# A conv-and-MLP trunk in split fp32 on one core: the activations' sums between stages are split in pieces from plain blocks, the input's gate product moves four steps

## The chip, the cores and the metric

The kernel runs on one core of one Trainium2 chip. Its time is device microseconds of that core, from one launch. The engines that matter are TensorE (PE for its matmuls, PEld for its weight loads), VectorE (DVE), ScalarE (ACT) and SyncE (SP), whose queue issues the DMAs. Every engine works through its own instructions in the order in which they were written; semaphores hold an instruction until what it needs is there.

## The reference

One layer: a gated short convolution and a squared-ReLU MLP, each after an RMS norm and added to the residual; 512 tokens, 2,048 channels, 8,192 hidden.

```python
h = rms_norm(x, norm_mix)
b_gate, c_gate, v = split(h @ conv_w_in, 3)          # 2048 x 6144
m = (b_gate * conv3(c_gate * v, conv_w)) @ conv_w_out # causal, depthwise, 3 taps
x = x + m
h = rms_norm(x, norm_mlp)
x = x + square(relu(h @ mlp_w1)) @ mlp_w2             # 2048 x 8192, 8192 x 2048
```

## The kernel before, in words

**Products.** Everything is fp32. Each operand is split into a high part, rounded to the type that PE multiplies in one pass, and a low part, the rest: `split` (L118) is a cast on ACT (L120) and a subtraction on DVE (L121). A product is three matmuls: high by high, high by low, low by high (L165 to L167 in plain blocks, L267 to L269 in fast blocks).

**Blocks and steps.** The output channels of each of the four weight matrices are worked off in blocks of 256 columns with 2,048 inputs. A *plain* block is 4 steps of 24 matmuls over 512 tokens each. A *fast* block is one level of Strassen-Winograd: inputs, outputs and tokens are halved, and 7 products of half size take the place of 8; it is 7 steps of 24 matmuls over 256 tokens each. Product by product the weights' quarters and sums are X11, S1, S2, S4, S3, X12, X22 (`quarters`, L169), and the activations' are Y11, T1, T2, Y22, T3, Y21, T4 (L33). In block 1 of a stage (`late`) the order is X11, X12, S2, S1, S3, S4, X22, so the activations' order is Y11, Y21, T2, T1, T3, Y22, T4.

The stages are `conv_w_in` (8 groups of the three parts C, V and B), `conv_w_out` (8 blocks), `mlp_w1` (32) and `mlp_w2` (4 times 8). The first, second and last block of `conv_w_in` behind the input, the first and last of `conv_w_out` and the first of `mlp_w1` are plain; the others are fast. There are 640 steps. Steps 0 to 3 and 4 to 7 are plain, 8 to 14 is the first fast block, (1,1) (group 1, part V); 141 to 144 is the last block of `conv_w_in`, 145 to 148 the first of `conv_w_out`; 191 to 194 its last, 195 to 198 the first of `mlp_w1`.

**Order.** It is written out by hand. At iteration i (L638 to L648) the kernel emits step i's matmuls, the copies out of PSUM of step i - 1 (`out`), the weight sums of step i + 3 (`add`), the weight split of step i + 2 (`operand`), and then what was put between steps with `at(i, ...)` (L203), in the order in which it was registered. So what is late on ACT or DVE in one iteration delays the copies and weights of the next ones. The products of a fast block add into three banks of PSUM; X11, S2, S3 and X22 share one, S1 and S4 another. The copy of one product must have left the bank before the next adds into it.

**Activations.** They lie in SBUF split, as quarters Y11, Y12, Y21, Y22 (`quart`), sums T2 and T4 (`sums`) and T3 (`last_sum`). T1 and Y12 share a place: plain blocks need all four quarters, fast blocks T1. Before a stage ends, its results go to DRAM by pairs of channel tiles (8 pairs), each with the four quarters and the four sums T1 to T4 (`differences`, L190; written by `keep`, L359). `pass_over` (L320) brings them into the next stage: with s the start of the last block and f that of the next stage's first, both plain, it reads and splits the quarters of pairs 0 to 6 (`fetch_pairs`, `settle_pairs`), takes the last pair's from its tile (`settle_last`), and then reads each sum as a whole, all eight pairs, from DRAM (`fetch`, L299) and splits it (`settle`, L304). Reads go into tiles of tag q, of which there are three; a read waits until its tile's last user is done, and SP's queue waits with it. The tag c, for a block's results, has two.

**The input.** While the first stage begins, the quarters are read back from DRAM (`fetch_h`, L570), normalised on ACT in eight operations (`normed_quarter`, L544), subtracted on DVE (`difference`, L574) and split (`settle_h`). `gate` (L389) multiplies a group's convolution by its B part on DVE, two operations of 1,024 columns, and appends the four sums (three operations); for group 0 that is registered for iteration 4. Y12, which the last block of `conv_w_in` needs again, is read 9 steps before it (L597).

In `residual` (L399) and `squared_relu` (L431) a finished block of `conv_w_out` or `mlp_w1` goes through DVE and ACT two iterations after its end. `token_factors` (L126) makes the second norm's factors: a matmul on PE at f + 2 = 197, then a chain on DVE with a square root on ACT.

Of the kernel before, what the change touches and what calls it, by code (L numbers as in the profile page):

```python
# [19 lines left out]
NP = KT // 2  # L20
# [3 lines left out]
NG = D // GC  # L24
# [8 lines left out]
Y11, T1, T2, Y22, T3, Y21, T4, Y12 = range(8)  # L33
PLACE = {Y11: 0, Y12: 1, Y21: 2, Y22: 3, T1: 4, T2: 5, T3: 6, T4: 7}
# [5 lines left out]
def trunk_kernel(  # L40
# [12 lines left out]
    nc = tc.nc  # L53
# [49 lines left out]
    sums = [cst.tile([P, 2, NP, HS], F32R, name=f"t_{n}") for n in ("hi", "lo")]  # L103
# [3 lines left out]
    def form(i):  # L107
        if i == T3:
            return last_sum
        return [quart[n][:, HOME[i]] if i in HOME else sums[n][:, i == T4] for n in range(2)]  # L110
# [7 lines left out]
    def split(hi, lo, src):  # L118

        act.copy(hi, src)  # L120
        dve.tensor_tensor(out=lo, in0=src, in1=hi.bitcast(F32), op=ALU.subtract)  # L121
# [68 lines left out]
    def differences(q):  # L190

        def tt(o, a, b):
            dve.tensor_tensor(out=q[:, o, :], in0=q[:, a, :], in1=q[:, b, :], op=ALU.subtract)

        tt(slice(4, 8, 2), slice(1, 4, 2), slice(0, 2))
        tt(5, 3, 4)
        tt(7, 2, 5)
# [5 lines left out]
    def at(i, fn, *args):  # L203
        between.setdefault(i, []).append((fn, args))
# [15 lines left out]
    def plain(w, r0, c0):  # L220
        box = new_block(w, r0, c0, KT // QK)

        def multiply(op, k0):
            if k0 == 0:
                box["acc"] = [bank() for _ in range(2)]
            plain_products(box["acc"], op, k0, k_first=True)

        def out(k0):
            if k0 == KT - QK:
                c = tile_c(box)  # L230
                for j in range(2):
                    act.copy(c[:, j, :], box["acc"][j])

        for k0 in range(0, KT, QK):
            steps.append((
                lambda: None,
                lambda k0=k0: plain_operand(box["r"], k0),
                lambda op, k0=k0: multiply(op, k0),
                lambda k0=k0: out(k0),
            ))  # L240
        return box
# [51 lines left out]
    def tile_q(name):  # L293
        return mw.tile([P, 8, HS], F32, tag="q", name=name, bufs=3)
# [22 lines left out]
    def settle_last(box):  # L317
        split(*(quart[i][:, :, NP - 1, :] for i in range(2)), box["q"][:, :4, :])

    def pass_over(last, first, src):  # L320


        s, f, box = last["start"], first["start"], {}
        at(s - 2, fetch_pairs, box, src, 0, 2)
        at(s, fetch_pairs, box, src, 2, 2)
        at(s + 1, settle_pairs, box, 0, 2)
        at(s + 1, fetch_pairs, box, src, 4, 2)
        at(s + 2, settle_pairs, box, 2, 2)
        at(s + 3, settle_pairs, box, 4, 2)
        at(s + 3, fetch_pairs, box, src, 6, 1)  # L330
        at(f, settle_pairs, box, 6, 1)
        at(f, settle_last, last)
        box = {}
        at(f + 1, fetch, box, src, T2)
        at(f + 2, fetch, box, src, T3)
        at(f + 3, settle, box, T2)
        at(f + 3, fetch, box, src, T1)
        at(f + 3, settle, box, T3)
        at(f + 3, fetch, box, src, T4)
        at(f + 4, settle, box, T1)  # L340
        at(f + 6, settle, box, T4)

    def exchange(start, src, reads):

# [11 lines left out]
    def tt(o, a, b, op):  # L356
        dve.tensor_tensor(out=o, in0=a, in1=b, op=op)  # L357
# [4 lines left out]
    def conv(n, box_c, box_v, d):  # L362

        e = box_v["end"]

        def product():
            tt(box_v["c"], box_c["c"], box_v["c"], ALU.mult)

        def factor():
            u = box_v["u"] = tile_x("u")  # L370
            dve.memset(u[:, :, 14:16], 0.0)
            tt(u[:, :, 16:], box_v["c"], wide(ssq), ALU.mult)

        def taps():
            u = box_v["u"]
            cv = box_v["cv"] = tile_x("cv")[:, :, :S]
            for j in range(2):
                act.activation(cv[:, j, :], u[:, j, 14 : 14 + S], AF.Copy, scale=tap(0, 2 * n + j))
                for i in (1, 2):
                    dve.scalar_tensor_tensor(  # L380
                        out=cv[:, j, :], in0=u[:, j, 14 + i : 14 + i + S], scalar=tap(i, 2 * n + j),
                        in1=cv[:, j, :], op0=ALU.mult, op1=ALU.add,
                    )

        at(e, product)
        at(e + d, factor)
        at(e + d + 1, taps)

    def gate(n, box_v, box, d):  # L389
        def product():  # L390
            q = box["q"] = tile_q("q")
            tt(box["c"], box["c"], box_v["cv"], ALU.mult)
            tt(q[:, :4, :].rearrange("p (i h) t -> p i (h t)", h=2), box["c"], wide(rbc), ALU.mult)

        at(box["end"] + d, product)
        at(box["end"] + d, lambda: differences(box["q"]))
        at(box["end"] + d + 1, keep, box, gated[n])
# [77 lines left out]
    with tc.tile_pool(name="xin", bufs=2) as xin:  # L475
# [18 lines left out]
        for c in range(D // XC):  # L494
# [5 lines left out]
            for i in range(2):  # L500
                src = w_in[c * XC : (c + 1) * XC, parts[i] : parts[i] + GC]
# [50 lines left out]
    for n in range(NG):  # L552
        trio = []
        for i in range(3):
            if n == 0 and i < 2:
                trio.append(boxes[i])
            elif (n, i) in ((0, 2), (1, 0), (NG - 1, 2)):
                trio.append(plain(w_in, 0, parts[i] + n * GC))
            else:
                trio.append(fast(w_in, 0, parts[i] + n * GC, late=(n, i) == (1, 1)))  # L560
            if i == 1:
                conv(n, *trio, 0 if n in (0, NG - 1) else 2)
        gate(n, *trio[1:], 0 if n in (0, NG - 1) else 2)
    in_last = trio[2]


# [1 line left out]
    hb = {}  # L568
# [17 lines left out]
    at(2, normed_quarter, hb, Y22)  # L586
    at(3, difference, Y12, Y22, Y12)
    at(3, settle_h, Y12, T3)
    at(4, difference, Y22, Y22, Y11)
    at(5, fetch_h, Y21)  # L590
    at(5, lambda: split(*form(T2), hb[Y22]))
    at(7, normed_quarter, hb, Y21)
    at(8, settle_h, Y11, T1)
    at(9, difference, Y21, Y21, Y22)
    at(10, settle_h, Y21, T4)

    at(in_last["start"] - 9, fetch_h, Y12)  # L597
    at(in_last["start"] - 6, normed_quarter, hb, Y12)
    at(in_last["start"] - 4, settle_h, Y12, Y12)


    for n in range(NG):
        if n in (0, NG - 1):
            box = plain(w_out, 0, n * GC)
        else:
            box = fast(w_out, 0, n * GC, late=n == 1)
        if n == 0:
            pass_over(in_last, box, gated)
        if n == NG - 1:
            back = {}  # L610
            at(box["start"] - 8, fetch, back, gated, Y12)
            at(box["start"] - 4, settle, back, Y12)
        residual(n, box, 0 if n >= NG - 2 else 2)


    for n in range(DFF // GC):
        last, box = box, fast(w1, 0, n * GC, late=n == 1) if n else plain(w1, 0, n * GC)
        if n == 0:
            pass_over(last, box, normed)
            at(box["start"] + 2, token_factors, lambda name: tile_x(name)[:, 0, :S])  # L620
        if n == DFF // GC - 1:
            exchange(box["start"], hidden[0], (-2, -1, 2, 3, 4, 5, 6))
        squared_relu(n, box)
    for ch in range(NCH):
        if ch:
            exchange(box["start"], hidden[ch], (-2, -1, 0, 2, 3, 4, 6))
        for n in range(NG):
            box = fast(w2, ch * D, n * GC)
# [53 lines left out]
```

## Time and profile before

| | us |
|---|---|
| median of 3 runs | 2005.88 (2002.95 to 2007.34) |
| the profiled execution | 2005.84 |
| its span, first to last instruction | 2004.1 |
| PE busy | 1932.6 (96%) |
| PEld busy | 1886.7 (94%) |
| DVE busy | 1650.9 (82%) |
| ACT busy | 979.5 (49%) |
| DMA | 355.79 MB, 178 GB/s on average |

In the page a matmul's duration overlaps its neighbours', so PE's busy time is not PE at its peak. The rows of a timeline give the start, the duration, the engine, the line of the kernel, the operation, what it writes and reads, and in brackets the engine's idle time before it with what ended it. The times of the 640 steps are not marked; they are found by the operands (q, t and u are `quart`, `sums` and `last_sum`) and the order above.

### The profile page before, as it was taken

The page shows a single profiled execution, that of the slowest core. Times are in us where ns is not written, and L with a number is a line of the kernel's source. Part 1 is how long each engine was busy: PE and PEld are TensorE (multiplying, and loading weights), DVE is VectorE, ACT ScalarE, POOL GpSimd, SP SyncE. Part 2 cuts the span into 40 slices and gives each one's busy share as a digit, 9 for nine tenths or more (in the row PEclk, how much of TensorE's full clock was granted, in tenths as well). Part 3 has the DMA queues.
Part 4 walks back from the last instruction along what each step waited for, and adds up shares of the span by engine and source line. Part 5 has one row for each costly group of instructions (what it writes and reads, how often), then busy time and mean ns, then how long its engine had stood idle before and what let it go on. Part 6 is the DMA issues. An engine that isn't in the chain of part 4 may idle for free. (4 is left out here: it accounts for less than half of the span.)

```text
span 2004.1 us, 36810 instructions
## 1 busy us (share of the span) xinstructions
PE 1932.6 (96%) x15729; PEld 1886.7 (94%) x15729; DVE 1650.9 (82%) x1686; ACT 979.5 (49%) x1232; POOL 0.7 (0%) x6
## 2 busy tenths in 40 slices
PE   9979999999989989999999999988999999999998
PEld 7769999999789879999999999988998998999998
DVE  6678988887688778888888888888889789879776
ACT  4544444444455544444544445454455446446443
POOL 0000000000000000000000000000000000000000
PEclk9999999999989989999999999999999999999999
DMA  8433433434755855445354453575556457548432
GB/s 273 168 126 112 142 130 103 148 106 170 266 184 198 306 177 171 152 165 180 136 190 152 164 181 135 190 250 177 183 198 243 159 188 265 178 149 291 161 136 96
DMA packets 279843, 355.79 MB, mean 178 GB/s; under 512 B 9520, under 2 KB 253312, under 8 KB 273536
## 3 DMA queue, kind: packets, MB, share of 16 engines
q1 hardware_dynamic: 279552, 353.41, 50.8%
q8 instruction: 123, 2.02, 0.4%
q14 instruction: 40, 0.33, 0.0%
q10 hardware_dynamic: 128, 0.04, 0.0%
HBM read 277.91 MB, written 75.50 MB: 176 GB/s over the span
## 5 line engine op out<-in xcount | busy, mean ns | idle before, releaser
L267 PE MATMUL acc<-q_hi,whi 128*128 128x256 f32 x2816 | 781.3, 277 | 4.0 <-ACT c L281 4.0
L269 PE MATMUL acc<-q_hi,wlo 128*128 128x256 f32 x2816 | 780.2, 277 | 2.6 <-DVE wlo L121 2.6
L268 PE MATMUL acc<-q_lo,whi 128*128 128x256 f32 x2816 | 780.5, 277 | 1.0 <-DVE q_lo L121 1.0
L121 DVE TENSOR_TENSOR wlo<-r,whi 128x1024 fp32r<-128x1024 f32 x384 | 469.2, 1222 | 232.2 <-ACT whi L120 222.6
L267 PEld LDWEIGHTS acc<-q_hi,whi 128*128 128x128 f32 x2816 | 531.1, 189 | 4.3 <-ACT c L281 4.2
L269 PEld LDWEIGHTS acc<-q_hi,wlo 128*128 128x128 f32 x2816 | 530.1, 188 | 3.1 <-DVE wlo L121 3.0
L268 PEld LDWEIGHTS acc<-q_lo,whi 128*128 128x128 f32 x2816 | 530.6, 188 | 1.9 <-DVE q_lo L121 1.8
L120 ACT CAST whi<-r 128x1024 fp32r<-128x1024 f32 x384 | 401.0, 1053 | 212.6 <-PE acc L268 115.8
L267 PE MATMUL acc<-t_hi,whi 128*128 128x256 f32 x1408 | 397.4, 282 | 32.8 <-DVE c L279 21.8
L269 PE MATMUL acc<-t_hi,wlo 128*128 128x256 f32 x1408 | 395.6, 281 | 2.2 <-DVE wlo L121 2.2
L268 PE MATMUL acc<-t_lo,whi 128*128 128x256 f32 x1408 | 395.5, 281 | 0.0
L120 ACT CAST whi<-s 128x1024 fp32r<-128x1024 f32 x264 | 278.4, 1055 | 206.0 <-DVE s L179 143.6
L121 DVE TENSOR_TENSOR wlo<-s,whi 128x1024 fp32r<-128x1024 f32 x264 | 322.3, 1221 | 25.9 <-ACT whi L120 22.2
L281 ACT COPY c<-acc 128x256 f32<-128x256 f32 x352 | 130.3, 370 | 402.2 <-PE acc L269 386.7
L267 PEld LDWEIGHTS acc<-t_hi,whi 128*128 128x128 f32 x1408 | 271.4, 193 | 35.1 <-issue 23.3
L269 PEld LDWEIGHTS acc<-t_hi,wlo 128*128 128x128 f32 x1408 | 270.9, 192 | 2.4 <-DVE wlo L121 2.4
L268 PEld LDWEIGHTS acc<-t_lo,whi 128*128 128x128 f32 x1408 | 271.1, 193 | 0.0
L267 PE MATMUL acc<-u_hi,whi 128*128 128x256 f32 x704 | 203.7, 289 | 13.5 <-ACT c L281 13.5
L268 PE MATMUL acc<-u_lo,whi 128*128 128x256 f32 x704 | 201.4, 286 | 1.3 <-DVE u_lo L121 1.3
L269 PE MATMUL acc<-u_hi,wlo 128*128 128x256 f32 x704 | 201.4, 286 | 0.0
L267 PEld LDWEIGHTS acc<-u_hi,whi 128*128 128x128 f32 x704 | 136.9, 195 | 14.7 <-ACT c L281 14.7
L268 PEld LDWEIGHTS acc<-u_lo,whi 128*128 128x128 f32 x704 | 137.0, 195 | 2.0 <-DVE u_lo L121 2.0
(76 smaller groups left out, 1796.7 us busy)
## 6 DMA issues: line engine op xcount, KB each, us to landing
r<-in_mlp_w_dram SPq DMA_DIRECT2D x256, 512.0 KB, 6.2
r<-in_conv_w_in_dram SPq DMA_DIRECT2D x96, 512.0 KB, 6.2
hidden<-q SPq DMA_DIRECT2D x32, 1024.0 KB, 4.3
f<-hidden SPq DMA_DIRECT2D x28, 1024.0 KB, 8.4
r<-in_conv_w_out_dram SPq DMA_DIRECT2D x32, 512.0 KB, 6.4
xt<-x_mid SPq DMA_DIRECT2D x32, 512.0 KB, 8.8
x_mid<-c SPq DMA_DIRECT2D x24, 512.0 KB, 2.6
gated<-q SPq DMA_DIRECT2D x8, 1024.0 KB, 3.8
```

What stands on the lines that cost most here:

```text
L120: act.copy(hi, src)
L121: dve.tensor_tensor(out=lo, in0=src, in1=hi.bitcast(F32), op=ALU.subtract)
L267: pe.matmul(acc, hi[:, k, :], f_hi[:, k, :], start=first, stop=False, skip_group_check=True)
L268: pe.matmul(acc, hi[:, k, :], f_lo[:, k, :], start=False, stop=False, skip_group_check=True)
L269: pe.matmul(acc, lo[:, k, :], f_hi[:, k, :], start=False, stop=last, skip_group_check=True)
L281: act.copy(o, acc)
```

## The change

Three parts.

1. In `pass_over`, pair 6 is read a step earlier in the order. Each sum is now read without its last pair (`fetch_most`: 7 of 8 pairs, one DMA of 896 KB), and split in two pieces: seven pairs from that read (`settle_most`) and the last pair from the tile in which it was made (`settle_rest`). Since the reads don't need the last pair in DRAM, they stand earlier: T2 at s + 3, T3 at f, T4 at f + 1, T1 at f + 2, in place of f + 1, f + 2, f + 3 (T1), f + 3 (T4). The splits stand at f + 1 (T2), f + 2 (T3), f + 3 (T4) and f + 4 (T1), in place of f + 3 (T2, T3), f + 4 (T1) and f + 6 (T4). The last pair's tile is in use until f + 4. This holds in both places that call `pass_over`.
2. At the input, Y21 is read at iteration 3 and not 5, and group 0's gate is registered for iteration 8 (its write to DRAM for 9) and not 4, behind T1's split.
3. Y12, before the last input block, is normalised and split one step later (5 and 3 steps before the block, not 6 and 4).

```diff
+    def fetch_most(box, src, i):
+        box[i] = tile_q("f")
+        nc.sync.dma_start(box[i][:, : NP - 1, :], src[: NP - 1, :, PLACE[i], :].rearrange("k p t -> p k t"))
+
+    def settle_most(box, i):
+        split(*(f[:, : NP - 1, :] for f in form(i)), box.pop(i)[:, : NP - 1, :])
+
+    def settle_rest(last, i):
+        split(*(f[:, NP - 1, :] for f in form(i)), last["q"][:, PLACE[i], :])
+
     def pass_over(last, first, src):
...
         at(s + 2, settle_pairs, box, 2, 2)
+        at(s + 2, fetch_pairs, box, src, 6, 1)
         at(s + 3, settle_pairs, box, 4, 2)
-        at(s + 3, fetch_pairs, box, src, 6, 1)
+        sums = {}
+        at(s + 3, fetch_most, sums, src, T2)
         at(f, settle_pairs, box, 6, 1)
         at(f, settle_last, last)
-        box = {}
-        at(f + 1, fetch, box, src, T2)
-        at(f + 2, fetch, box, src, T3)
-        at(f + 3, settle, box, T2)
-        at(f + 3, fetch, box, src, T1)
-        at(f + 3, settle, box, T3)
-        at(f + 3, fetch, box, src, T4)
-        at(f + 4, settle, box, T1)
-        at(f + 6, settle, box, T4)
+        at(f, fetch_most, sums, src, T3)
+        at(f + 1, settle_most, sums, T2)
+        at(f + 1, settle_rest, last, T2)
+        at(f + 1, fetch_most, sums, src, T4)
+        at(f + 2, settle_most, sums, T3)
+        at(f + 2, settle_rest, last, T3)
+        at(f + 2, fetch_most, sums, src, T1)
+        at(f + 3, settle_most, sums, T4)
+        at(f + 3, settle_rest, last, T4)
+        at(f + 4, settle_most, sums, T1)
+        at(f + 4, settle_rest, last, T1)
...
-        gate(n, *trio[1:], 0 if n in (0, NG - 1) else 2)
+        if n:
+            gate(n, *trio[1:], 0 if n == NG - 1 else 2)
+        else:
+            first_trio = trio
...
     at(3, settle_h, Y12, T3)
+    at(3, fetch_h, Y21)
     at(4, difference, Y22, Y22, Y11)
-    at(5, fetch_h, Y21)
     at(5, lambda: split(*form(T2), hb[Y22]))
     at(7, normed_quarter, hb, Y21)
     at(8, settle_h, Y11, T1)
+    gate(0, *first_trio[1:], 4)
     at(9, difference, Y21, Y21, Y22)
     at(10, settle_h, Y21, T4)

     at(in_last["start"] - 9, fetch_h, Y12)
-    at(in_last["start"] - 6, normed_quarter, hb, Y12)
-    at(in_last["start"] - 4, settle_h, Y12, Y12)
+    at(in_last["start"] - 5, normed_quarter, hb, Y12)
+    at(in_last["start"] - 3, settle_h, Y12, Y12)
```

## The prediction, made before the changed kernel ran

> **What bounds the kernel now.** I read the page first, then the stages' windows, then PE's timeline for its pauses, and last the timelines of ACT, DVE and SP around each pause. First the page's first line, then two windows of 300 and 3 us (columns: stretch, its length, busy time with count for PE, PEld, DVE, ACT, POOL, then granted clock, DMA share, GB/s).
>
> ```profile
> span 2004.1 us, 36810 instructions
> ```
>
> ```profile
> 150.00:450.00 300.00, 300.00 (x2627) 300.00 (x2626) 265.12 (x284) 140.21 (x185) 0.00 (x0) 1.00 0.36 124
> 552.90:555.90 3.00, 2.96 (x14) 2.96 (x15) 3.00 (x2) 0.94 (x1) 0.00 (x0) 0.50 0.08 29
> ```
>
> In the fast blocks PE never pauses: 300/2627 is 0.114 us a matmul, 2.73 us a step of 24; a plain step, 24 matmuls twice as wide, some 5.5. Right after a pause the clock is 0.50: 3/14 is 0.214 us a matmul. So time is to be had only where PE pauses. PE's timeline, the pauses that the change can reach (idle time in brackets):
>
> ```profile
> 110.26 0.50 PE L167 MATMUL acc<-q_hi,wlo 128*128 128x512 f32 x1 [1.51 <-DVE wlo L121]
> 128.64 0.58 PE L267 MATMUL acc<-t_hi,whi 128*128 128x256 f32 x1 [7.32 <-ACT c L281]
> 485.15 0.58 PE L267 MATMUL acc<-q_hi,whi 128*128 128x256 f32 x1 [3.98 <-ACT c L281]
> 552.94 0.58 PE L267 MATMUL acc<-t_hi,whi 128*128 128x256 f32 x1 [3.64 <-ACT c L281]
> 564.89 0.39 PE L267 MATMUL acc<-u_hi,whi 128*128 128x256 f32 x1 [3.39 <-ACT c L281]
> 727.46 0.39 PE L269 MATMUL acc<-q_hi,wlo 128*128 128x256 f32 x1 [2.40 <-DVE wlo L121]
> 744.82 0.58 PE L267 MATMUL acc<-u_hi,whi 128*128 128x256 f32 x1 [4.57 <-ACT c L281]
> ```
>
> They sum to 26.8 us, and a pause costs more than itself. Groups of L267, first in 673.3 to 676.0, then in 1668.3 to 1671.0, two pauses that the change leaves alone: after 2.1 us idle a matmul takes 286 ns, after 2.4 us it takes 449.
>
> ```profile
> L267 PE MATMUL acc<-t_hi,whi 128*128 128x256 f32 x8 | 2.3, 286 | 2.1 <-DVE c L279 2.1
> L267 PE MATMUL acc<-t_hi,whi 128*128 128x256 f32 x4 | 1.8, 449 | 2.4 <-DVE c L279 2.4
> ```
>
> The releaser "ACT c L281" is a copy out of PSUM: the next product adds into the same bank and must wait for it. ACT is in order, so a copy is late when something ahead of it waits.
>
> **The input.** DVE, then ACT, then SP:
>
> ```profile
> 102.75 1.22 DVE L357 TENSOR_TENSOR c<-c,cv 128x1024 f32<-128x1024 f32 x1
> 104.00 1.23 DVE L357 TENSOR_TENSOR q<-c,rbc 128x1024 f32<-128x1024 f32 x1
> 105.26 1.61 DVE L193 TENSOR_TENSOR q<-q 128x512 f32<-128x512 f32 x3
> 106.79 2.28 DVE L357 TENSOR_TENSOR f<-f 128x2048 f32<-128x2048 f32 x1
> 108.99 1.22 DVE L121 TENSOR_TENSOR wlo<-r,whi 128x1024 fp32r<-128x1024 f32 x1
> ...
> 136.50 1.22 DVE L121 TENSOR_TENSOR wlo<-r,whi 128x1024 fp32r<-128x1024 f32 x1
> ```
>
> ```profile
> 121.33 3.30 ACT L547 ACTIVATE f<-f,par 128x256 f32<-128x256 f32 x8 [8.36 <-DMA f<-x_res]
> ```
>
> ```profile
> 110.24 2.02 SPq L146 DMA_DIRECT2D r<-in_conv_w_in_dram  x4
> 112.36 0.48 SPq L572 DMA_DIRECT2D f<-x_res  x1
> ```
>
> Gate 0 (102.75 to 106.79, 4.04 us) stands ahead of step 7's low weights (108.99), and the read of Y21 stands behind four weight loads that wait for those; ACT waits 8.36 us for it, and with it the copies. With gate 0 gone from step 4, the low weights are done 4.04 us sooner, at 106.2; step 7 has no pause, and ends 1.7 sooner at 113.7 (110.26 + 22 x 0.23 - 1.7; to the idle time a little of matmul is added). Y21's read goes out when T3's low half frees its tile, just before the next low weights at 101.6; it is normalised before 113.7 if it lands within 8.7 us.
>
> Gate 0's new place brings a new wait. Tag c has two buffers, and the copy of block (1,1)'s X11 at iteration 9 wants the one that gate 0's product reads at iteration 8. From 113.9: two copies 1.0, S2's high weights 1.0, T1's high half 1.9 (117.75), its low half 2.29 (120.0), the product's two operations 1.25 each (122.5), the copy 0.37: step 10 (S2) starts at 122.9, where 119.2 (113.7 + 2 x 2.73) would be free and 128.64 was before. Behind that DVE runs differences 1.6, S3's addition 1.14, low weights 1.14, T4's difference 2.2, an addition 0.34, S4's addition 1.14, and reaches step 12's low weights (before: 136.50) at 130.0. **I take 6.5.** Low end 1.7 (only the first pause goes), high end 9.4 (the copy finds a free buffer).
>
> **Y12 before the last input block.** ACT, then PE:
>
> ```profile
> 481.55 3.30 ACT L547 ACTIVATE f<-f,par 128x256 f32<-128x256 f32 x8 [4.45 <-DMA f<-x_res]
> 484.75 0.35 ACT L281 COPY c<-acc 128x256 f32<-128x256 f32 x1
> ```
>
> ```profile
> 490.44 0.41 PE L267 MATMUL acc<-u_hi,whi 128*128 128x256 f32 x1
> ```
>
> The normalisation waits for its read, and S1's copy (484.75) behind it holds step 137. One step later, S1's copy is ahead of it; step 137 follows step 136 at once, and now S2's copy stands behind, at the same 484.75, and holds step 138 (S3) until 485.15 instead of 490.44: **5.3**. Behind 484.75 come the copy 0.27, two high weights 1.9, Y12's high half 1.9 and low half 2.3: 491.2; step 141 reads them from 485.15 + 3 x 2.73 = 493.3. Low end 2.7 (one step, if the rest keeps the half clock), high 6.9 (pause and half clock wholly gone).
>
> **First transition (f = 145).** SP, then the page's group of these reads (median us from issue to landing), then ACT and DVE:
>
> ```profile
> 532.28 0.37 SPq L302 DMA_DIRECT2D f<-gated  x1
> 532.70 0.61 SPq L403 DMA_DIRECT2D xt<-x_res  x1
> 533.41 3.82 SPq L146 DMA_DIRECT2D r<-in_conv_w_out_dram  x4
> 537.27 7.12 SPq L302 DMA_DIRECT2D f<-gated  x3
> ```
>
> ```profile
> f<-gated SPq DMA_DIRECT2D x5, 1024.0 KB, 9.7
> ```
>
> ```profile
> 547.00 1.91 ACT L120 CAST u_hi<-f 128x2048 fp32r<-128x2048 f32 x1 [6.03 <-DMA f<-gated]
> ```
>
> ```profile
> 528.24 1.22 DVE L121 TENSOR_TENSOR q_lo<-f,q_hi 128x1024 fp32r<-128x1024 f32 x1
> ...
> 552.65 2.29 DVE L121 TENSOR_TENSOR q_lo<-f,q_hi 128x2048 fp32r<-128x2048 f32 x1 [0.28 <-ACT q_hi L120]
> ```
>
> T2's read (532.28) waits until the last pair is written, T3's (537.27) stands behind the loads, and ACT waits for it until 547.00; X11's copy, behind its cast and others, releases step 151 at 552.94. After, T2 is read into the tile that frees when pairs 2 and 3 are split, two steps before f, and T3 into pair 6's, free at 529.5 (528.24 + 1.22). The last pair's tile is held to f + 4, so T4 takes T2's tile: behind pair 6 DVE has the last pair's 1.14, weights 1.14 and T2's 1.95, so 533.6. T1 takes T3's, which lands at 529.5 + 5.2 (the least of such reads, quoted with the rivals) and is split by 538.3. T4's read makes SP wait and the loads behind it go out 1.1 us later; their first use is at step 153, some 20 us on. T1's read goes out last, behind the loads, so it gets the median of 9.7, less 0.3 for the missing eighth: 538.3 + 9.4 = 547.7. Casts 1.9: X11's copy ends near 549.9, step 151 starts at 550.0 instead of 552.94.
>
> The second pause is another one. From T1's low half (552.65) DVE goes through S3, weights, S4, weights and T4 (2.2) to the residual's sum; two ACT scalings wait for that, S2's copy for those, and step 153 (564.89) for the copy: 12.24 us. T1's low half now starts near 549.4 and T4 is gone ahead, so step 153 starts at 549.4 + 12.24 - 2.2 = 559.4, with the pieces 559.5: **5.4**, bounds 1 (T1 lands 4 us later) to 8.5 (T1 never late). About 3 us of the second pause stays.
>
> Splits: no row has a 1,792 wide or a 256 wide one. 1,024 columns take DVE 1.22 and 2,048 take 2.29, so a piece has some 0.15 of its own, of which successors hide a part; the 256 wide copy (0.35) bounds it above, 0 below. I take 0.1 a pair and engine, near the 0.15; the eight pairs are in these sums.
>
> **Second transition (f = 195).** DVE:
>
> ```profile
> 716.44 0.69 DVE L132 TENSOR_SCALAR m<-acc 128x512 f32<-128x512 f32 x1 [4.38 <-PE acc L130]
> ...
> 727.33 2.28 DVE L121 TENSOR_TENSOR t_lo<-f,t_hi 128x2048 fp32r<-128x2048 f32 x1
> 729.53 2.28 DVE L121 TENSOR_TENSOR u_lo<-f,u_hi 128x2048 fp32r<-128x2048 f32 x1
> ```
>
> From the end of the token factors DVE is the path, without a hole, to the squared ReLU; its square on ACT and S2's copy follow, and then step 203 (744.82). T2's and T3's low halves (2.2 each) leave this chain for a time before the factors, when DVE waited for PE's token sum (4.38 us idle ahead of 716.44); T4's only changes place. 2 x 2.2 is 4.4, less 0.2 for pieces and 0.3 because T3's last piece may run into the factors: **3.9**, bounds 0 (T3's read lands 4 us late, and ACT's square root waits) to 7 (T4 too leaves the chain). Step 203 starts at 740.9.
>
> Reading pair 6 a step earlier costs and brings nothing: in both transitions SP already waited for its tile or queue.
>
> **Sum.** 6.5 + 5.3 + 5.4 + 3.9 = 21.1. The profiled run took 2005.84 us, 1.7 beside the span, and the median is 2005.88: **1984.7**.
>
> **Rivals.**
> - The clock stays full after the shorter rests at S3 (3 and 2.8 us): 14 matmuls in 3 us at 0.214 instead of 0.114 are 1.4 us, twice: 1981.9. The 2.4 us row above, at 449 ns, speaks against it. [...]
> - Only the input gains: S2's copy stays where it is because DVE's and ACT's order, not the reads, sets it: 6.5 + 5.3, 1994.0. For it: at 564.89 no DMA is the releaser. Against: T4's split stands in that chain.
> - Gate 0 at step 8 gives back what it frees (1.7 left): 1989.5. For it: the c buffer.
> - All these pauses vanish, with their half clock: 26.8 + six times 1.4: 1970.6. Against: the residual and the ReLU stay in the chain.
> - Slower: the reads queue up. T3 to T1 and T2 to T4 go one after another through two tiles. All reads of L302:
>
> ```profile
> DMA to landing us min/median/max: 5.2/8.8/13.5
> ```
>
>  If Y21, T3 and T1 each took 13.5 us, Y21 would normalise 4.5 late (input -2); T1's cast would start at 529.5 + 13.5 + 3.6 + 13.5 = 560, and step 151 near 562.4, 9.4 later than before; T3 would push the token factors by 8 (net +4). With Y12's 5.3: about 2011.5. It decides from some 12 us a read; the reads now go out where DMA has less to do.
> - The reads go out no earlier, because their tiles come free no sooner: within 0.2%. SP's place of pair 6 shows such waits.
>
> **Chances.** Forecast 0.47 (own range 1979 to 1990), clock 0.06, input alone 0.18, gate 0 0.11, all gone 0.06, slower 0.07, nothing 0.05. Range 1976 to 1999: it takes in the low ends' sum but 1.4 us (1.7 + 2.7 + 1 + 0 = 5.4, 2000.4) and leaves out the last three. About 0.2% (4 us) is what can be told from no change: faster 0.88, same 0.06, slower 0.06.
>
> **What would show it.** Right: no pause in step 7; ACT's normalisation of Y21 before block (1,0)'s copies; a pause of some 3.7 us at S2 of (1,1), ended by a copy that waits for gate 0; Y12's pause at S3, some 1.5 us; T2's and T3's low halves before PE's token sum; about 3 us left at both S3. Wrong: an ACT wait for a DMA in either transition over 3 us, or a pause in a block that had none.

## The result, and the profile after

The changed kernel takes 1983.43 us (median of 3 runs, 1983.15 to 1983.49) where the kernel before takes 2005.88: a ratio of 0.9894, 95% interval 0.988 to 0.9908. The profiled run took 1983.15 us.

The page's first line, and PE's timeline at its pauses where the change acts, those that the forecast turns on (idle time in brackets):

```profile
span 1981.4 us, 36826 instructions
```

```profile
123.44 0.58 PE L267 MATMUL acc<-t_hi,whi 128*128 128x256 f32 x1 [2.95 <-ACT c L281]
478.08 0.39 PE L267 MATMUL acc<-u_hi,whi 128*128 128x256 f32 x1 [0.26 <-ACT c L281]
540.59 0.38 PE L267 MATMUL acc<-t_hi,whi 128*128 128x256 f32 x1 [2.74 <-ACT c L281]
544.67 0.38 PE L269 MATMUL acc<-q_hi,wlo 128*128 128x256 f32 x1 [0.87 <-DVE wlo L121]
550.09 0.39 PE L267 MATMUL acc<-u_hi,whi 128*128 128x256 f32 x1 [2.63 <-ACT c L281]
710.95 0.39 PE L269 MATMUL acc<-q_hi,wlo 128*128 128x256 f32 x1 [2.77 <-DVE wlo L121]
718.90 0.39 PE L269 MATMUL acc<-q_hi,wlo 128*128 128x256 f32 x1 [1.45 <-DVE wlo L121]
724.05 0.38 PE L267 MATMUL acc<-u_hi,whi 128*128 128x256 f32 x1 [2.36 <-ACT c L281]
```

The pause in step 7 is gone. The input's large one fell from 7.32 to 2.95, Y12's from 3.98 to 0.26, and those at S3 of the two transitions from 3.39 and 4.57 to 2.63 and 2.36. The one at S2 of the first transition is nearly as long as before (3.64, now 2.74). In the second transition the pause at 710.95 was 2.40 before; one of 2.16 in the step of S2 (at 733.00 before) is down to 0.39, and one of 1.45 has come in the next step.

Pauses don't show how far the run has come ahead, because a chain of work can hold PE through clock and pause alike. For that I take the same instruction in both traces and subtract its starts. ACT's weight casts (and one copy) at six marks, before and then after: the start of the input, ahead of the first transition, behind it, ahead of the second, behind it, and the last one of all:

```profile
92.88 1.03 ACT L120 CAST whi<-r 128x1024 fp32r<-128x1024 f32 x1
...
538.11 1.05 ACT L120 CAST whi<-r 128x1024 fp32r<-128x1024 f32 x1 [4.55 <-PE acc L166]
...
574.99 0.37 ACT L281 COPY c<-acc 128x256 f32<-128x256 f32 x1 [1.73 <-PE acc L269]
...
709.75 1.05 ACT L120 CAST whi<-r 128x1024 fp32r<-128x1024 f32 x1 [1.81 <-PE acc L166]
...
766.25 2.00 ACT L120 CAST whi<-r 128x1024 fp32r<-128x1024 f32 x2
...
1987.34 1.05 ACT L120 CAST whi<-r 128x1024 fp32r<-128x1024 f32 x1 [1.28 <-PE acc L268]
```

```profile
93.83 1.03 ACT L120 CAST whi<-r 128x1024 fp32r<-128x1024 f32 x1
...
526.66 1.05 ACT L120 CAST whi<-r 128x1024 fp32r<-128x1024 f32 x1 [0.74 <-PE acc L166]
...
558.71 0.37 ACT L281 COPY c<-acc 128x256 f32<-128x256 f32 x1 [1.66 <-PE acc L269]
...
692.87 1.05 ACT L120 CAST whi<-r 128x1024 fp32r<-128x1024 f32 x1
...
743.14 2.00 ACT L120 CAST whi<-r 128x1024 fp32r<-128x1024 f32 x2
...
1964.64 1.05 ACT L120 CAST whi<-r 128x1024 fp32r<-128x1024 f32 x1 [1.29 <-PE acc L268]
```

After minus before, the marks read +0.95, -11.45, -16.28, -16.88, -23.11 and -22.70. Input and Y12 together bring 12.4, the first transition 4.8, the second 6.2; the rest of the run adds next to nothing. The 0.95 is lost before the first mark, where no edit acts.

### The profile page after: what moved, and what is told of

The parts are those of the page before. It is cut to its first block, busy times and chain, and to the rows that moved or that the text cites. A ratio compares the mean times of both kernels' runs of the same rounds, so it can differ in the third digit from the quotient of the medians.

```text
span 1981.4 us, 36826 instructions
## 1 busy us (share of the span) xinstructions
PE 1920.8 (97%) x15729; PEld 1874.0 (95%) x15729; DVE 1650.1 (83%) x1694; ACT 981.2 (50%) x1240; POOL 0.7 (0%) x6
## 3 DMA queue, kind: packets, MB, share of 16 engines
q8 instruction: 123, 2.02, 0.4%
```

## The experiments

Times of one group were taken beside the same runs of the kernel before; its medians were 2004.94, 2004.59 and 2004.75 us in the three groups.

**Only the input** (part 2 of the change).

```diff
-        gate(n, *trio[1:], 0 if n in (0, NG - 1) else 2)
+        if n:
+            gate(n, *trio[1:], 0 if n == NG - 1 else 2)
+        else:
+            first_trio = trio
...
+    at(3, fetch_h, Y21)
-    at(5, fetch_h, Y21)
+    gate(0, *first_trio[1:], 4)
```

> Only the input's part of the change: gate 0 at iteration 8 and Y21's read at 3; Y12 and both transitions as before. Theory (each part acts in its own place): no pause in step 7, S2 of block (1,1) waits some 3 us for a copy that waits for gate 0, and everything behind is 6.5 us earlier: 1999.3, with 2 us either way for where the half clock falls. Rival (the reads in the transitions or Y12 profit only because the input is earlier): the gain here would be some other number, over 10 or under 3.

Measured: 1997.96 us, ratio 0.9964 (0.9952 to 0.9977).

**Only Y12 later** (part 3).

```diff
-    at(in_last["start"] - 6, normed_quarter, hb, Y12)
-    at(in_last["start"] - 4, settle_h, Y12, Y12)
+    at(in_last["start"] - 5, normed_quarter, hb, Y12)
+    at(in_last["start"] - 3, settle_h, Y12, Y12)
```

> Only Y12's normalisation and split one step later. Theory: S1's copy is ahead of the normalisation, the pause moves from step 137 (4 us and half clock) to step 138 (about 1.5 us): 5.3 us less, 2000.5. Rival (the split of Y12 comes too late for the plain block at step 141, so the wait only moves): a new pause at step 141, and less than 2 us gained, 2004 or more.

Measured: 2001.56 us, 0.9983 (0.9974 to 0.9991). The trace has 5.5 us at the place itself, but the medians differ by only 3.4, and the interval is 1.8 to 5.2 us: the time alone does not confirm 5.3.

**Only the transitions** (part 1: `pass_over` and its three new functions).

```diff
+        at(s + 3, fetch_most, sums, src, T2)
...
+        at(f, fetch_most, sums, src, T3)
+        at(f + 1, settle_most, sums, T2)
+        at(f + 1, settle_rest, last, T2)
...
```

> Only the new transitions; the input and Y12 as before. Theory: 9.3 us by the forecast's terms (5.4 and 3.9), and up to 2 more where a pause keeps full clock: 1994 to 1997. Rival (S2's copy is held by DVE's and ACT's order alone): no gain, 2004 or more.

Measured: 1996.12 us, 0.9955 (0.9941 to 0.9969). The three parts alone take 0.36%, 0.17% and 0.45%, in sum 0.98%, beside 1.06% of the whole: within the intervals they add, and none needs another.

**Group 0's gate late, but Y21 read as before** (half of part 2).

```diff
-        gate(n, *trio[1:], 0 if n in (0, NG - 1) else 2)
+        if n:
+            gate(n, *trio[1:], 0 if n == NG - 1 else 2)
+        else:
+            first_trio = trio
...
     at(5, fetch_h, Y21)
+    gate(0, *first_trio[1:], 4)
```

> Only gate 0 at iteration 8; Y21's read stays at 5, Y12 and the transitions as before. Theory: the read still stands behind the four weight loads, now issued near 107 to 109, so Y21 lands near 118 and is normalised until 122; then two copies, S2's weights and T1's high half (125.6), T1's low half (127.9), gate 0's product (130.4) and the copy of X11: step 10 starts near 130.8, 2 us later than before, and the pause of step 7 is gone all the same. In total 1 to 2 us slower than before, 2007. Rival (gate 0 ahead of step 7's weights was the cost, the read a side matter): step 10 near 123 to 125 and 4 us or more faster, 2002 or less.

Measured: 2005.38 us, 0.9999 (0.999 to 1.0007), no change; of the 1 to 2 us of loss that had been expected, at most 1.4 lies in the interval. ACT's and PE's timelines of this kernel:

```profile
119.02 3.31 ACT L547 ACTIVATE f<-f,par 128x256 f32<-128x256 f32 x8 [7.26 <-DMA f<-x_res]
...
130.83 0.37 ACT L281 COPY c<-acc 128x256 f32<-128x256 f32 x1 [4.81 <-DVE q L357]
```

```profile
131.25 0.58 PE L267 MATMUL acc<-t_hi,whi 128*128 128x256 f32 x1 [9.36 <-ACT c L281]
```

Step 7 no longer pauses, but ACT still waits 7.26 us for Y21's read, and then the copy waits 4.81 for the gate that now stands behind T1's split. Step 10 starts at 131.25, where it was 128.64. So the gate's move alone only changes the place of the wait, and with the earlier read it is a gain: 7.0 us with it, nothing without it. The earlier read alone, with the gate where it was, was not run; how much of the 7.0 it would bring without the gate's move is open.

**The changed kernel again**, beside the three that follow.

> The changed kernel itself once more, beside the next three on one chip: 1983.4 as before, with the same 2 to 3 us pauses. Theory of the clock: whether such a pause is followed by half clock depends on where it falls, so the same pauses may cost up to 2 us more or less each in another execution.

Measured: 1984.98 us, 0.9903 (0.9889 to 0.9916). Its trace differs from the first in one thing that matters here. ACT in the first transition, at T1:

```profile
539.88 1.68 ACT L120 CAST q_hi<-f 128x1792 fp32r<-128x1792 f32 x1 [6.03 <-DMA f<-gated]
```

T1's read, issued at 528.35, came 11.5 us later and not 9.4 as in the first trace. S2 paused 4.47 us and started 0.8 later than in the kernel before (with the 11.59 that the run was ahead set off), and the first transition brought 3.1 by the marks, not 4.8; the second brought 6.3, as in the first trace.

**T1's read ahead of the weight loads.** The loads of the third block of `conv_w_out` and of `mlp_w1` go out one step later, so that they no longer stand before T1's read.

```diff
-        at(loads[-2]["end"] - LEAD - 1 if len(loads) > 1 else -1, ...)
+        d = int((w is w_out or w is w1) and r0 == 0 and c0 == 2 * GC)
+        at(loads[-2]["end"] - LEAD - 1 + d if len(loads) > 1 else -1, ...)
```

> The changed kernel, but the four weight loads of the third block of both new stages stand one iteration later, behind T1's read and not ahead of it. Theory (T1 was the last to land and held S2 of the first transition): T1 goes out near 527.7 instead of 528.9 and lands near 534 instead of 538; S2's pause of 2.9 goes, S3 starts 4 us sooner, nothing changes in the second transition, where the token factors set the pace: 1979.3. Rival (T1 is late because its tile is late, or because DMA is full anyway): it lands no more than 1 us sooner and the time stays within 1 us of the changed kernel's.

Measured: 1982.01 us, 0.9888 (0.9874 to 0.9901). SP and ACT of this kernel (its lines from L212 on are numbered one higher, and it runs 2.2 us behind the changed kernel when it comes here):

```profile
530.05 0.38 SPq L324 DMA_DIRECT2D f<-gated  x1
530.48 3.28 SPq L146 DMA_DIRECT2D r<-in_conv_w_out_dram  x4
```

```profile
536.08 1.69 ACT L120 CAST q_hi<-f 128x1792 fp32r<-128x1792 f32 x1
```

The read goes out 1.0 us sooner, when T3's split has freed its tile, lands before ACT wants it, and the pause at S2 is gone. So it was T1's read, late behind the loads, that set S2. A pause of 1.99 us stays at S3, and here the clock halved behind it (from 549.14 the matmuls start 0.21 us apart, where they had been 0.12), which gave part back: 2.9 us are left behind the transition. The intervals of this kernel and of the changed one overlap.

**Half of the gate earlier.** The first of the two operations of group 0's gate product at iteration 6, the second still at 8.

```diff
+        if n == 0:
+            at(box["end"] + d - 2, convolved)   # c <- c * cv
         at(box["end"] + d, product)
```

> The changed kernel, but of gate 0's product the first operation (the convolution times the B part, 1,024 columns) stands two iterations earlier, at 6, where DVE waits; the second stays at 8. Theory (the copy of X11 waits for gate 0's last reading of its buffer, and DVE's chain behind sets step 12): the copy and step 10 come 1.2 us sooner, and so does everything behind: 1982.2. Rival (the copy is held by something else): no change at step 10.

Measured: 0.9899 (0.9883 to 0.9915), no difference that can be told. In its trace S2's pause of the input is 1.81 instead of 2.95, which is the operation that was moved; but the copies ahead of it came 1.35 us later in this run, and step 10 started at 123.65, no sooner than the 123.44 of the changed kernel. The clock tells the two apart: here it was 0.50 from 104.26 to 107.67 (matmuls 0.43 us apart), where the changed kernel's trace has 1.00 (0.23 apart).

**The reads early, the splits where they were.** The order of the reads is the new one as far as the tiles allow, the splits stand at f + 3 (T2, T3), f + 4 (T1) and f + 6 (T4).

```diff
-        at(f + 1, settle_most, sums, T2)
...
+        at(f + 3, settle_most, sums, T2)
...
+        at(f + 3, fetch_most, sums, src, T1)
+        at(f + 3, settle_most, sums, T3)
...
+        at(f + 6, settle_most, sums, T4)
```

> The changed kernel, but T2 and T3 are split at f + 3, T1 at f + 4 and T4 at f + 6, as in the kernel before; T2's and T3's reads stay early and without the last pair, those of T1 and T4 go to f + 3 since their tiles come free there. Theory (the second transition's gain is the low halves' early place on DVE, not the reads): 4 us lost again in the second transition; in the first T4's low half is back in the chain to S3 and T1 lands later, some 4 us lost: 1991.5. Rival (the early reads bring it): 1986 or less.

Measured: 1993.98 us, 0.9942 (0.9929 to 0.9955). In its second transition, PE at S2, then ACT at T1:

```profile
725.90 0.58 PE L267 MATMUL acc<-t_hi,whi 128*128 128x256 f32 x1 [4.85 <-ACT c L281]
```

```profile
723.59 1.68 ACT L120 CAST q_hi<-f 128x1792 fp32r<-128x1792 f32 x1 [6.92 <-DMA f<-normed]
```

It gives back most of what the transitions brought (0.39% of 0.45%), 1.8 us in the first and 8.6 in the second by the traces (against the changed kernel's second trace nothing in the first). So the early reads of T2 and T3 are worth little while their splits stand late. Why is only in part shown. The low halves are back behind the token factors, as expected, and S3's pause is 3.79; but T2's late split also holds the tile into which T1 is read (the read goes out at 718.69, as that split ends), and the wait for it makes the pause at S2, which the kernel before did not have. The run does not separate the two.

**The first residual and the first squared ReLU one step later** (with their sums and writes), to free S2's copy from the scalings that stand before it on ACT.

```diff
-        residual(n, box, 0 if n >= NG - 2 else 2)
+        residual(n, box, 0 if n >= NG - 2 else 3 if n == 0 else 2)
...
+        d = int(n == 0)
-        at(box["end"] + 2, product)
+        at(box["end"] + 2 + d, product)
...
```

> The changed kernel, with the residual of the first conv_w_out block and the squared ReLU of the first mlp_w1 block one step later (three steps after the block's end, not two; their sums and writes one step later too). In the profile of the changed kernel the pauses at S3 of both transitions, 2.80 and 2.53 us, end with the copy of S2's product, which ACT reaches only after the scalings or the square, and these wait for DVE's addition at 547.14 or its maximum at 721.36. Theory (the order on ACT holds the copy): now the copy stands ahead of them and is done when S2's matmuls are, both pauses go, 2.80 + 2.53 = 5.3 us less, near 1979.5 beside 1984.9 for the changed kernel, ratio to the kernel before near 0.988. Rival 1 (the pause moves one step): the scalings now hold S3's copy and the next product in that bank, and nothing is gained, ratio 0.990. Rival 2 (DVE is the path: the sums of the residual, 1.6 us, now fall among the weights of later steps): slower by up to 1.6 us a place, ratio 0.992.

Measured: 1983.14 us, 0.9892 (0.9878 to 0.9907). ACT and PE of the first transition:

```profile
550.08 1.33 ACT L426 ACTIVATE q<-xt,par 128x512 f32<-128x512 f32 x2 [2.43 <-DVE xt L373]
```

```profile
551.73 0.38 PE L267 MATMUL acc<-q_hi,whi 128*128 128x256 f32 x1 [0.99 <-ACT c L281]
```

S3 starts without a pause in both transitions, as the theory has it. But rival 1 takes over, with another copy than it had named: the scalings now stand before S1's, and S4, which adds into S1's bank, waits. Against the changed kernel the traces have 0.8 us in the first transition and nothing in the second. The order of the ACT work is a cause of the pause, but DVE's addition, for which the scalings still wait 2.43 us, stays.

**Both, and all three.** The later residual and ReLU with T1's read first, and then also half of the gate earlier.

> The kernel with the later residual and ReLU, and the weight loads of the third block of conv_w_out and mlp_w1 behind T1's read. Theory: the two act on different pauses of the first transition (S2's, 2.90 us, which T1's read holds, and S3's, 2.80, which the copy holds), so they add: 5.3 + 2.9 = 8.2 us less than the changed kernel, near 1976.7, ratio near 0.986. Rival: both shorten one chain, the one that ends in S2's copy, and the second to be taken away gives at most 1 us more than either alone: 1979.0, ratio 0.987 or above.

> The same, and the first operation of group 0's gate product two steps earlier, which alone shortened the pause of the input by 1.1 us in the trace and changed nothing measurable in the time. Theory: 1.1 us less than without it, 1975.6. Rival: what it gains at step 10 comes back in the input's later steps, 1976.7 as without it. The two lie within what this measurement can tell, so the trace decides, by when step 14 starts.

Measured: 1977.18 us, 0.9863 (0.9847 to 0.988), and 1978.36 us, 0.987 (0.9856 to 0.9885). Both beat the kernel before. The changed kernel did not run in this group, so against it only the ratios can be compared: the intervals of the two lie below that of its second group of runs (0.9889 to 0.9916); that of its first (0.988 to 0.9908) the first one touches, and the second one overlaps a little. That they are faster than the changed kernel is likely by this, and not shown beyond doubt. PE of the first of them, at S4, the only pause of 0.7 us or more that is left in the first transition's block, where the changed kernel paused 2.74 and 2.63 us at S2 and S3:

```profile
548.97 0.39 PE L268 MATMUL acc<-q_hi,whi 128*128 128x256 f32 x1 [0.76 <-ACT c L282]
```

By the marks the traces of both show 5.1 us of gain over the changed kernel's first trace in the first transition, more than the two edits brought alone in theirs (2.9 and 0.8); in the second there is again none. Against the changed kernel's second trace, where T1's read came later, it is 6.9. The ratios differ by 5 to 8 us. Between the two kernels the times show no difference; in the traces step 14 starts 44.2 us behind the first mark with the gate's operation moved and 45.4 without, as the theory has it.

## Why the prediction was right, point by point

The forecast was 1984.7 us, the time 1983.4. Its four terms, and what the marks and pauses give for them:

| | forecast | measured |
|---|---|---|
| input | 6.5 | 7.0 |
| Y12 | 5.3 | 5.4: 6.3 at S3, 0.9 lost behind it |
| first transition | 5.4 | 4.8: 3.3 at S3, 1.5 of clock |
| second transition | 3.9 | 6.2: 3.9 at S3, 2.3 of clock |
| sum | 21.1 | 23.4; the marks have 23.65 from the first to the last, 22.7 with the 0.95 lost ahead of them |

**Input.** A window over step 7 (columns as in the prediction), then ACT, then DVE:

```profile
108.50:113.90 5.40, 5.40 (x25) 4.36 (x24) 5.37 (x5) 4.68 (x10) 0.00 (x0) 1.00 0.92 289
```

```profile
110.05 3.31 ACT L563 ACTIVATE f<-f,par 128x256 f32<-128x256 f32 x8
114.18 1.28 ACT L232 COPY c<-acc 128x512 f32<-128x512 f32 x2 [0.82 <-PE acc L167]
...
123.02 0.37 ACT L281 COPY c<-acc 128x256 f32<-128x256 f32 x1 [4.81 <-DVE q L373]
```

```profile
121.70 1.23 DVE L373 TENSOR_TENSOR q<-c,rbc 128x1024 f32<-128x1024 f32 x1
...
130.43 1.22 DVE L121 TENSOR_TENSOR wlo<-r,whi 128x1024 fp32r<-128x1024 f32 x1
```

Each sign that was named is there, the pause at S2 with 2.95 us where some 3.7 had been named. PE is busy through step 7 at full clock; Y21 is normalised at 110.05 without a wait and ahead of the copies at 114.18; X11's copy waits 4.81 us for the second operation of the gate, and S2 of (1,1) starts at 123.44, forecast 122.9 and the 0.95 of the start, 123.85. Step 12's low weights stand at 130.43 instead of 136.50. With the start that is 7.0.

**Y12.** ACT, then PE at step 140 and DVE ahead of it:

```profile
474.46 3.31 ACT L563 ACTIVATE f<-f,par 128x256 f32<-128x256 f32 x8 [0.72 <-DMA f<-x_res]
```

```profile
484.54 0.35 PE L267 MATMUL acc<-t_hi,whi 128*128 128x256 f32 x1 [0.58 <-DVE c L279]
```

```profile
481.76 2.29 DVE L121 TENSOR_TENSOR q_lo<-f,q_hi 128x2048 fp32r<-128x2048 f32 x1
```

S1's copy now stands ahead of the normalisation, as worked out, and PE no longer waits at step 137. But the sign named for step 138, a pause of some 1.5 us, is 0.26, and 0.17 in the run of Y12 alone. That the 5.4 is so near the 5.3 is luck: two things that the forecast did not have set each other off. Y12's read was ready 9.9 us after its issue and not 10.9 (9.8 in the run of Y12 alone), so S3 starts 6.3 us sooner (490.44 to 478.08, less the 6.1 of the input). Then step 140 waits for S3's addition, which on DVE stands behind Y12's low half (481.76, and the addition at 483.97), and 0.9 of it is lost again by the plain block's start.

**First transition.** SP, then ACT, then DVE:

```profile
523.48 5.29 SPq L146 DMA_DIRECT2D r<-in_conv_w_out_dram  x4
528.87 1.79 SPq L323 DMA_DIRECT2D f<-gated  x1
```

```profile
538.27 1.68 ACT L120 CAST q_hi<-f 128x1792 fp32r<-128x1792 f32 x1 [4.29 <-DMA f<-gated]
```

```profile
539.99 2.02 DVE L121 TENSOR_TENSOR q_lo<-f,q_hi 128x1792 fp32r<-128x1792 f32 x1 [4.75 <-ACT q_hi L120]
```

The term that was mis-sized is T1's read. The forecast let it go out at 538.3, which is 526.85 with the 11.45 that the run was ahead, and take 9.4 us. In this trace it took 9.4 (528.87 to 538.27), but went out 2.0 later: T3's split freed its tile 0.8 later (527.68), and the four weight loads before it, which kept SP for 5.29 us and not for the 3.82 of the row before, held it for the other 1.2. In the second trace of this kernel the read itself took 11.5, and S2 gained nothing. ACT's wait of 4.29 us is the sign that had been named as "wrong", and it was right to name it: S2 started 0.9 us sooner, and not 2.9. Behind that the chain is as worked out: from T1's low half to S3 it takes 10.10 us (539.99 to 550.09), where 12.24 less 2.2 for T4 is 10.04 and the pieces 0.1. S3 is 3.3 sooner. The kernel with T1's read first showed the cause by taking it away: there the read lands within 6.03 us. The pause of 0.87 at 544.67, in a step that had none before, is the same lateness once more: DVE came to those weights only behind T1's low half.

**Second transition.** DVE:

```profile
693.56 2.02 DVE L121 TENSOR_TENSOR t_lo<-f,t_hi 128x1792 fp32r<-128x1792 f32 x1
...
697.66 2.02 DVE L121 TENSOR_TENSOR u_lo<-f,u_hi 128x1792 fp32r<-128x1792 f32 x1 [0.61 <-ACT u_hi L120]
...
699.94 0.68 DVE L132 TENSOR_SCALAR m<-acc 128x512 f32<-128x512 f32 x1
```

Both low halves lie ahead of the token factors and delay them a little: m starts 16.50 us sooner than before (716.44), where the run was 16.88 ahead; 0.3 had been set for that. S3 starts 20.77 sooner: 3.9, the forecast.

**The clock.** The rest came from the rival with a chance of 0.06. Windows behind S3's pause in the two transitions, before and then after:

```profile
565.80:568.80 3.00, 3.00 (x17) 3.00 (x16) 2.98 (x4) 2.15 (x3) 0.00 (x0) 0.50 0.61 254
745.20:748.20 3.00, 3.00 (x16) 3.00 (x16) 2.39 (x4) 1.73 (x3) 0.00 (x0) 0.50 0.03 5
```

```profile
550.30:553.30 3.00, 3.00 (x27) 3.00 (x26) 2.90 (x6) 2.98 (x5) 0.00 (x0) 1.00 0.35 150
724.20:727.20 3.00, 3.00 (x26) 3.00 (x27) 2.19 (x3) 2.01 (x4) 0.00 (x0) 1.00 0.02 5
```

Pauses of 2.63 and 2.36 us kept the full clock here: 27 and 26 matmuls in 3 us where there had been 17 and 16. Ten matmuls are 1.1 us of a window; from S3's start to the mark behind it, it comes to 1.5 and 2.3. So the forecast was near the time with one term 2 us short at S3 of the first transition and a rival's gain of 3.8 us on the other side: that it came within 1.3 us is in part luck. This gain isn't the change's to keep: it turns on where the pause falls, as the last section shows. In the run with T1's read first the pause at S3 of the first was 1.99 us, shorter than these two, and the clock halved behind it.

**The other rivals.** That only the input gains is refuted by the run of the transitions alone (0.9955). That gate 0 gives back what it frees is what the gate's move does without the read; with the read it doesn't. The pauses didn't all vanish. The reads didn't queue up; all reads of the new function, both transitions:

```profile
DMA to landing us min/median/max: 5.8/7.1/9.4
```

That is below the 12 us at which this rival was to decide, though one read of the second trace (11.5) came near it. (The terms that the prediction names for this rival add up to 2011.9, where it has about 2011.5.)

## What to carry to other kernels

Work that is split off for the next stage belongs where its engine waits anyway; reading it early was worth little here while it was still split late. When one of two waits on an in-order engine is moved, look for the other one: the gate's move was worth nothing until Y21's read moved too, and S3's pause went on to S4 when only ACT's order was changed. A read that is on the critical path should be issued ahead of bulk loads that are needed later, since here the loads held both the queue (SP for 5.29 us) and the transfer (9.4 us from issue to use behind them, 6.03 ahead of them).

## What the runs showed of the hardware

**A pause of the same length halves the clock or doesn't.** In `mlp_w2`, which no edit touches, there are three places where a block waits for the same addition. The trace before has the halved clock at all three (granted clock 0.61, 0.50 and 0.50 in the 3 us behind the pause), the changed kernel's at none (1.00), and that of the kernel with T1's read first at all three again (0.66, 0.63 and 0.52). The prediction had taken such rows for a threshold between 2.1 and 2.4 us; that was wrong: a pause of 2.40 us is among those with the halved clock and among those without. PE's timeline at the first place, before: the end of the pause and the start of the slow stretch.

```profile
1507.22 0.36 PE L267 MATMUL acc<-t_hi,whi 128*128 128x256 f32 x1 [2.74 <-DVE c L279]
...
1507.89 0.39 PE L269 MATMUL acc<-t_hi,wlo 128*128 128x256 f32 x1
```

PE works on at full speed from 1507.22, and the slow stretch starts at 1507.89: the change comes at a time of its own, not at the pause's end. The clock in the traces says when. From 100 us to the last 5 the trace before has 12 slow stretches and the changed kernel's 4. Each lasts 3.41 us or twice that, and starts a whole multiple of 3.413 us behind the first one of its trace, to within 3 ns, wherever the pauses fall. So in these traces the clock changes on a grid of 3.413 us that the pauses don't shift. Two neighbouring windows of that grid at the second place, before and then after:

```profile
1664.92:1668.33 3.41, 1.05 (x10) 0.86 (x8) 3.41 (x4) 0.00 (x0) 0.00 (x0) 1.00 1.03 377
1668.33:1671.74 3.41, 3.37 (x16) 3.40 (x17) 3.41 (x4) 2.27 (x2) 0.00 (x0) 0.50 1.08 383
```

```profile
1641.48:1644.89 3.41, 2.38 (x21) 2.18 (x20) 3.41 (x4) 1.22 (x2) 0.00 (x0) 1.00 1.01 357
1644.89:1648.31 3.42, 2.05 (x18) 2.08 (x19) 3.42 (x5) 0.96 (x1) 0.00 (x0) 1.00 1.06 383
```

The pause is 2.40 us of idle time in both. Before, it falls almost whole into one window (busy for 1.05 us, idle for 2.36), and the next window is slow; after, two windows share it (1.03 and 1.37 idle), and the clock stays full.

The pauses at S3 of the two transitions were shared in this way too (1.76 and 0.88, 1.61 and 0.75 idle). Over the 1,138 windows of the grid at full clock in the two traces, before and after, none with 1.81 us of idle PE or less was followed by a slow one, and every one with 1.91 or more was. That is no figure for every run: in the plain blocks at the start some 1.53 us, in two pauses, was enough in four other traces (the gate's move alone, half of the gate earlier, and the two of "Both, and all three").

What a slow stretch costs depends on what is behind it. At the second place it cost nothing: from the pause's end to the next pause for the addition it is 23.57 us with it (1668.37 to 1691.94) and 23.55 without (1646.26 to 1669.81). Behind S3 of the transitions it cost the 1.5 and 2.3 us named above. Why the times of one kernel's runs spread by some us is open.

**Four issues held SP for 2 to 5 us.** Four weight loads took SP 5.29 us in the first transition of the changed kernel (quoted above), 3.82 in that of the kernel before and 2.02 ahead of Y21's read (both quoted in the prediction); the mean busy share of the DMA engines was 1.03, 0.99 and 0.35 there. Where the DMA engines were full the issues took longer; with T1's read first they took 3.28 (quoted above). What sets their length beyond that is not shown. T1's read took 9.4 us from issue to ACT's cast behind the loads. In the kernel that issues it first, ACT found it landed 6.03 us after its issue (530.05 to 536.08) without a wait.

**The rounded type takes one row.** In the trace before, a product of two rounded operands over 512 tokens is one row of PE, and the next starts 0.23 us behind it (715.15 to 715.38). The token sum of `token_factors`, one product in plain fp32, is two rows, at 715.38 and 715.81.
